# Small tiles moved behind the large ones: every large SBUF tile starts on a multiple of 512 bytes

## The chip, the cores and the metric

One core of one Trainium2 chip runs the whole program in one launch. The metric is the device time of that core in microseconds (us).

## The reference, cut to what matters

Two layers over x (256 positions, 1,024 channels, float32), each of three sub-layers with an RMS norm before and after:

```python
for i in range(DEPTH):                      # 2
    h = swiglu(rms_norm(x, g[0]), w_gate, w_up, w_down)      # D_FF = 2816
    x = x + 0.5 * rms_norm(h, g[1])
    hm = rms_norm(x, g[2])
    m = dilated_attention(hm, ...) if i == 0 else retention(hm, ...)
    x = x + rms_norm(m, g[3])
    h = swiglu(rms_norm(x, g[4]), w_gate, w_up, w_down)
    x = x + 0.5 * rms_norm(h, g[5])
```

Every weight is read once from HBM, and every product with a weight has 256 rows, so the work is one long stream of weights through TensorE.

## The kernel before, in words

**The weight stream.** Class `Stream` (L26 to L131) loads weights in groups of 1 MB into tiles `raw` (two buffers, 8,192 bytes per partition), issued by SP in `dma`. `split` cuts a group into two pieces of 128x1024 and writes each piece twice: ScalarE makes `hi` (L109, L115), rounded to fp32r, and VectorE makes the rest, `lo` (L110, L116). The pieces lie in rings of six tiles each, tags `whi` and `wlo`. When a piece has been used, `done` makes the next. Fourteen pieces at the borders of the sub-layers go to the idle tags C0, C1 and C2 instead (`wx`; `run` lists them, three per border and two behind the attention).

**The products.** `mm3` (L182 to L184) multiplies in three passes: (x high, w high), (x high, w low), (x low, w high). In each the 128x128 block of x is the stationary operand, loaded into the array by an LDWEIGHTS of its own, and 512 columns of the weights are the moving one. A triple below is these three. x high and x low are `xh` and `xl` in the first product of each sub-layer, `hh` and `hl` (tags A and B) in the down products of the feed-forward parts, `ot` (tags E0, E1 and C0) in the attention's output product, and `zh` and `zl` (tags A and B) in the retention's. Counted from the loops, there are 5,160 such matmuls: 4 x 528 in the feed-forward units (result tiles `ac`), 864 in the attention's (`at`), 768 in the retention's (`rt`), 4 x 264 + 96 + 192 = 1,344 in the down products (`d_f`, `d_at`, `d_rt`), and 72 in `rt_y` (tile `y`), where the stationary operand is `s` (tags x0 and x1) and the moving one `vv` (tag C1). Of those in the units, 14 x 12 = 168 have a `wx` as moving operand. Transposes, scores and softmax are separate matmuls of other lines.

**The order of the work.** It is the program's order on each queue; `enter` and the tail of `down` fix the order of PE, DVE and ACT by hand. Piece by piece, PE consumes what ACT and DVE have split; a piece ahead is split when one is done with.

**Where the tiles lie.** All SBUF tiles come from one pool, `sb` (L148). A tag's place is given when its first tile is asked for, one behind the other, each size rounded up to 32 bytes; the pool begins at byte 4,224 of the partition, which is 128 behind a multiple of 512. The large tiles have sizes that are multiples of 512, but tiles of 4 to 128 bytes (`rstd`, `ss2`, `nwt`, `pn`, `m`, `den`, ...) and `gcol` (384 bytes) lie between them. Adding up the sizes gives these starts, as the rest by 512:

| tiles | before | after |
|---|---|---|
| x0, x1 (also `s`), sg, raw, ident | 128 | 0 |
| xh, xl (blocks of x within them at 0 or 256) | 0 | 0 |
| whi, wlo | 64 | 0 |
| tmpa, pr | 128 | 0 |
| gpost, A, B (hh, hl, zh, zl, PT), E0, E1 (ot), C0, C1, C2 (wx, vv, qk), h, D | 224 | 0 |
| tmpb | 320 | 0 |

Of the kernel before, what the change touches and what calls it, by code (L numbers as in the profile page):

```python
# [6 lines left out]
F32 = mybir.dt.float32  # L7
# [7 lines left out]
P = 128  # L15
# [125 lines left out]
class Trunk:  # L141
    def __init__(self, tc, aps, out, ctx):
        self.tc, self.nc, self.out = tc, tc.nc, out
        self.__dict__.update(aps)
        self.pend = []
        self.bg = []
        self.begun = False
        self.sb = ctx.enter_context(tc.tile_pool(name="sb", bufs=1))  # L148
        self.ps = ctx.enter_context(tc.tile_pool(name="ps", bufs=6, space=PSUM))
        self.pt = ctx.enter_context(tc.tile_pool(name="pt", bufs=2, space=PSUM))  # L150
        self.dram = ctx.enter_context(tc.tile_pool(name="dram", bufs=1, space=DRAM))
# [6 lines left out]

    def setup(self):
        nc, sb = self.nc, self.sb  # L160

        self.x = [sb.tile([P, D], F32, tag=f"x{t}", name=f"x{t}") for t in range(2)]
        xr = self.x_in[0].rearrange("(i r) d -> r i d", r=4)
        gr = sb.tile([96, P], F32, tag="sg", bufs=2, name="gr")
        nc.sync.dma_start(gr, self.norm_gains.rearrange("l n (k p) -> (l n k) p", p=P))
        for t in range(2):
            for rr in range(2):
                nc.sync.dma_start(self.x[t][rr * 64 : rr * 64 + 64, :], xr[2 * t + rr])
            self.ws.dma(halves=t == 0)
        self.ident = sb.tile([P, P], F32, name="ident")  # L170
        make_identity(nc, self.ident)
        warm = self.acc("warm")
        for _ in range(WARM):
            nc.tensor.matmul(warm[:, :P], self.ident, self.ident, start=True, stop=True)
        tr = self.trb("gtr")
        nc.tensor.transpose(tr[:, :96], gr, self.ident[:96, :96])
        self.gcol = sb.tile([P, 96], F32, name="gcol")
        nc.vector.tensor_copy(self.gcol, tr[:, :96])

    def mm3(self, out, xh, xl, wh, wl, start, stop):  # L180
# [22 lines left out]
    def rsqrt(self, ss, name, mean, out=None):  # L203

        nc, n = self.nc, ss.shape[1]
        t = self.sb.tile([P, 4 * n], F32, tag="nwt%d" % n, bufs=3, name=f"nw_{name}")
        v, y, u, r = (t[:, i * n : i * n + n] for i in range(4))
        nc.vector.tensor_scalar(out=v, in0=ss, scalar1=mean, scalar2=EPS, op0=ALU.mult, op1=ALU.add)
        self.newton(v, y, u)
        r = r if out is None else out  # L210
        nc.vector.tensor_scalar(out=r, in0=y, scalar1=1.0 / NEWTON, scalar2=None, op0=ALU.mult)
        return r
# [14 lines left out]
    def pre_alloc(self, name):  # L227
        self.xh = self.sb.tile([P, NK, XC], F32R, tag="xh", name=f"xh_{name}")
        self.xl = self.sb.tile([P, NK, XC], F32R, tag="xl", name=f"xl_{name}")
        self.rstd = self.sb.tile([P, 2], F32, tag="rstd", bufs=2, name=f"rstd_{name}")  # L230

    def pre_sums(self, name, t, ss=None):
        if ss is None:
            ss = self.sb.tile([P, 2], F32, tag="ss2", bufs=2, name=f"ss_{name}")
        junk = self.sb.tile([P, D], F32, tag="tmpa", bufs=1, name=f"sq_{name}_{t}")
        if name == "in":
            self.nc.vector.scalar_tensor_tensor(out=junk, in0=self.x[t], scalar=1.0, in1=self.x[t], op0=ALU.mult, op1=ALU.mult, accum_out=ss[:, t : t + 1])
        else:
            self.nc.scalar.activation(junk, self.x[t], AF.Square, accum_out=ss[:, t : t + 1])
        return ss  # L240
# [7 lines left out]
    def post(self, t, banks, gb, name):  # L248

        nc, sb = self.nc, self.sb  # L250
        w = sb.tile([P, 5], F32, tag="pn", bufs=3, name=f"pn_{name}_{t}")
        junk = sb.tile([P, 512], F32, tag="tmpb", bufs=1, name=f"psq_{name}_{t}")
        yg = sb.tile([P, D], F32, tag="tmpa", bufs=1, name=f"yg_{name}_{t}")
        for h in range(2):
            s = slice(h * 512, h * 512 + 512)
            nc.scalar.activation(junk, banks[h], AF.Square, scale=2.0**-5, accum_out=w[:, h : h + 1])
            nc.vector.tensor_tensor(out=yg[:, s], in0=banks[h], in1=gb[:, s], op=ALU.mult)
        v, y, u = (w[:, i : i + 1] for i in (2, 3, 4))
        nc.vector.scalar_tensor_tensor(out=v, in0=w[:, 0:1], scalar=EPS, in1=w[:, 1:2], op0=ALU.add, op1=ALU.add)
        self.newton(v, y, u)  # L260
        for h in range(2):
            s = slice(h * 512, h * 512 + 512)
            nc.vector.scalar_tensor_tensor(out=self.x[t][:, s], in0=yg[:, s], scalar=y, in1=self.x[t][:, s], op0=ALU.mult, op1=ALU.add)
# [266 lines left out]
    def attn(self, plan, nxt):  # L530
        nc, sb = self.nc, self.sb
# [3 lines left out]
        rq = ru = None  # L535
        tasks_o1 = None
        for u, (o, kind, g, pieces) in enumerate(plan["units"]):
# [2 lines left out]
                bias, loads = self.bias_load(o)  # L540
            if u == 0:
                self.first_unit(pieces, accs)
                rq = sb.tile([P, 2], F32, tag="rq", name="rq")
                nc.vector.tensor_scalar(out=rq, in0=self.rstd, scalar1=-0.125, scalar2=None, op0=ALU.mult)
                for z in (self.xh, self.xl):
                    nc.gpsimd.tensor_copy(z[:, :, 256:320], z[:, :, 0:64].bitcast(F32))
                tr = self.trb("rut")
                nc.tensor.matmul(tr[0:64, 0:2], self.ident[:, 64:128], self.rstd, start=True, stop=True)
                nc.tensor.matmul(tr[64:128, 0:2], self.ident[:, 0:64], self.rstd, start=True, stop=True)
                ru = sb.tile([P, 2], F32, tag="ru", name="ru")  # L550
                nc.vector.tensor_copy(ru[0:64, :], tr[0:64, 0:2])
                nc.vector.tensor_copy(ru[64:128, 0:1], tr[64:128, 1:2])
                nc.vector.tensor_copy(ru[64:128, 1:2], tr[64:128, 0:1])
            else:
                for _ in range(2):
                    if loads:
                        loads.pop(0)()
                self.unit(pieces, accs, cols=(64, 192) if (kind == "v" and g == 2) else (0, P))
            if kind != "v":
# [4 lines left out]
                w = 0 if kind == "q" else 1  # L564
# [3 lines left out]
                    self.pend.append(lambda t=t, nat=nat, dst=qk[g][:, w, :, t * P : (t + 1) * P], u=u, w=w: self.qk_store(t, nat, dst, u, w == 0))  # L568
                if kind == "k" and g == 2:
                    st = dict(o=o, qk=qk, bias=bias, PT=sb.tile([P, 16, 384], F32, tag="B", name=f"PT{o}"),  # L570
                              den=sb.tile([P, 2, 16], F32, tag="den", bufs=2, name=f"den{o}"))

                    def push(st=st):
                        n = 8
                        for j in range(n + 2):
                            def step(j=j):
                                if j < n:
                                    self.sm_scores(st, j)
                                if 1 <= j <= n:
                                    self.sm_exp(st, j - 1)  # L580
                                if j >= 2:
                                    self.sm_trans(st, j - 2)
                            self.bg += [step, lambda: None]
                    self.pend.append(push)
# [49 lines left out]
    def sm_scores(self, st, j):  # L634


        nc, sb = self.nc, self.sb
# [13 lines left out]
        for s in range(2):  # L651
            i = 2 * j + s
            pr = sb.tile([P, 384], F32, tag="pr", bufs=6, name=f"pr{st['o']}_{i}")
            m = sb.tile([P, 1], F32, tag="m", bufs=6, name=f"m{st['o']}_{i}")
            nc.vector.tensor_tensor_reduce(
                out=pr.rearrange("p (b c) -> p b c", c=64), in0=sc[s][:, :384].rearrange("p (b c) -> p b c", c=64),
                in1=st["bias"][:, 4 * T : 4 * T + 6, i % 8, :], scale=1.0, scalar=3.0e38, op0=ALU.add, op1=ALU.min, accum_out=m)
            st["pr", i], st["m", i] = pr, m
# [206 lines left out]
    def rt_gate(self, st, d, sg):  # L865

        nc, sb = self.nc, self.sb
        h = st["h"]
        mv = sb.tile([P, 2, 2], F32, tag="mv", bufs=2, name=f"mv{h}{d}")
        for t in range(2):  # L870
            bs = sb.tile([P, 6], F32, tag="bs", bufs=2, name=f"bs{h}{d}{t}")
            nc.vector.bn_stats(out=bs, in_=st["y", d][t])
            nc.vector.bn_aggr(out=mv[:, t, :], in_=bs)
        r = self.rsqrt(mv[:, :, 1], f"gn{h}{d}", 1.0)
        for t in range(2):
            if d == 0:
                w = st["C2"][:, 512 * t : 512 * t + 512]
# [82 lines left out]
```

## Time and profile before

| | us |
|---|---|
| median of 3 runs | 1318.09 (1317.95 to 1318.52) |
| the profiled execution, its own time | 1317.18 |
| its span, first to last instruction | 1315.1 |
| PE busy | 1298.9 |
| VectorE (DVE) busy | 864.7 |
| ScalarE (ACT) busy | 712.1 |

The profile is one execution; 2.1 us of its own time lie outside the span. Matmuls overlap in the records: one of 512 columns is shown as some 390 to 400 ns long, while the next begins some 230 ns after it. So the busy share of PE and a matmul's length say little of its rate; the distance from one start to the next does, and the timeline shows it, in hundredths of a microsecond.

### The profile page before, as it was taken

How to read it: one execution, taken by the hardware profiler on the slowest of the kernel's cores; microseconds unless marked ns; L12 is line 12 of the kernel's file. 1: busy time of each engine (PE TensorE's matmuls, PEld its weight loads, DVE VectorE, ACT ScalarE, POOL GpSimd, SP SyncE). 2: the span in 40 equal slices, each digit the busy share in tenths (PEclk: the TensorE clock that was granted, in tenths of full speed). 3: DMA queues.
4: the chain of work that ended last, by engine and by line, in shares of the span. 5: the costliest groups of instructions: out<-in, count | busy, mean ns of one | idle time of the engine just before them, and what ended most of it. 6: DMA issues, size and time to landing. Idle time of an engine off the chain costs nothing.

```text
span 1315.1 us, 16640 instructions
## 1 busy us (share of the span) xinstructions
PE 1298.9 (99%) x6326; PEld 1051.8 (80%) x6326; DVE 864.7 (66%) x1541; ACT 712.1 (54%) x1103; POOL 19.4 (1%) x16
## 2 busy tenths in 40 slices
PE   8999999999999999999999999999999999999997
PEld 6878887877887778888888888877888887888886
DVE  5765547678467768765476665588787875766544
ACT  4655444566555658764455654455554545565532
POOL 1000001000000000000000000000000000000000
PEclk9999999999999999999999999999999999999999
DMA  7755467855864346554546555545454545565551
GB/s 214 235 183 192 173 212 183 203 192 147 204 179 158 129 149 227 192 192 173 184 162 227 170 189 192 192 144 185 152 175 145 176 160 192 166 202 183 172 190 64
DMA packets 129691, 235.45 MB, mean 179 GB/s; under 512 B 25019, under 2 KB 41899, under 8 KB 129612
## 3 DMA queue, kind: packets, MB, share of 16 engines
q1 hardware_dynamic: 129468, 234.14, 56.0%
q8 instruction: 49, 0.80, 0.2%
q10 hardware_dynamic: 144, 0.26, 0.1%
q14 instruction: 30, 0.25, 0.1%
HBM read 232.21 MB, written 1.12 MB: 177 GB/s over the span
## 4 chain that ended last, share of the span: by engine, by line
PE 90%; DVE 4%; DMA 3%; ACT 2%; issue 1%; SPq 0%; DVEq 0%; ACTq 0%
PE ac_f L184 12%; PE ac_f L183 12%; PE ac_f L182 12%; PE d_f L182 6%; PE d_f L184 6%; PE d_f L183 6%; PE at L182 5%; PE at L184 5%; PE at L183 5%; PE rt L184 4%; PE rt L183 4%; PE rt L182 4%; PE htr L340 1%; DMA raw<-in_ret_w_in_dram 1%; DMA raw<-in_ffn_w_gate_dram 1%; PE ptt L676 1%
## 5 line engine op out<-in xcount | busy, mean ns | idle before, releaser
L116 DVE SCALAR_TENSOR_TENSOR wlo<-raw,gcol,whi 128x512 fp32r<-128x512 f32 x596 | 417.2, 747 | 191.2 <-ACT whi L115 190.6
L115 ACT ACTIVATE whi<-raw,gcol 128x512 fp32r<-128x512 f32 x596 | 393.8, 715 | 273.2 <-PE ac_f L184 87.1
L110 DVE TENSOR_TENSOR wlo<-raw,whi 128x1024 fp32r<-128x1024 f32 x112 | 137.2, 1225 | 144.9 <-ACT whi L109 144.7
L109 ACT ACTIVATE whi<-raw 128x1024 fp32r<-128x1024 f32 x112 | 118.7, 1060 | 172.2 <-PE d_f L184 103.3
L182 PE MATMUL d_f<-whi,hhf 128*128 128x512 f32 x352 | 140.7, 400 | 0.0
L184 PE MATMUL d_f<-whi,hlf 128*128 128x512 f32 x352 | 138.8, 394 | 0.0
L183 PE MATMUL d_f<-wlo,hhf 128*128 128x512 f32 x352 | 138.2, 393 | 0.0
L182 PE MATMUL at<-whi,xh_f 128*128 128x512 f32 x276 | 111.6, 404 | 0.0
L184 PE MATMUL at<-whi,xl_f 128*128 128x512 f32 x276 | 108.3, 392 | 0.0
L183 PE MATMUL at<-wlo,xh_f 128*128 128x512 f32 x276 | 107.4, 389 | 0.0
L183 PE MATMUL rt<-wlo,xh_f 128*128 128x512 f32 x244 | 97.1, 398 | 0.0
L182 PE MATMUL rt<-whi,xh_f 128*128 128x512 f32 x244 | 96.7, 396 | 0.0
L184 PE MATMUL rt<-whi,xl_f 128*128 128x512 f32 x244 | 96.4, 395 | 0.0
L184 PEld LDWEIGHTS d_f<-whi,hlf 128*128 128x128 f32 x352 | 66.1, 188 | 17.1
L183 PEld LDWEIGHTS d_f<-wlo,hhf 128*128 128x128 f32 x352 | 66.1, 188 | 15.4
L182 PEld LDWEIGHTS d_f<-whi,hhf 128*128 128x128 f32 x352 | 66.1, 188 | 15.1
L182 PE MATMUL ac_f<-whi,xh_in 128*128 128x512 f32 x176 | 70.4, 400 | 2.2 <-ACT whi L115 1.9
L183 PE MATMUL ac_f<-wlo,xh_in 128*128 128x512 f32 x176 | 69.1, 392 | 1.2 <-DVE wlo L116 1.2
L184 PE MATMUL ac_f<-whi,xl_in 128*128 128x512 f32 x176 | 69.3, 394 | 0.0
L184 PE MATMUL ac_f<-whi,xl_at 128*128 128x512 f32 x168 | 66.2, 394 | 0.0
L182 PE MATMUL ac_f<-whi,xh_at 128*128 128x512 f32 x168 | 65.8, 393 | 0.2 <-ACT xh_at L224 0.2
L183 PE MATMUL ac_f<-wlo,xh_at 128*128 128x512 f32 x168 | 65.9, 392 | 0.0
(290 smaller groups left out, 2162.8 us busy)
## 6 DMA issues: line engine op xcount, KB each, us to landing
raw<-in_ffn_w_down_dram SPq DMA_DIRECT2D x44, 1024.0 KB, 4.9
raw<-in_ffn_w_up_dram SPq DMA_DIRECT2D x40, 1024.0 KB, 5.1
raw<-in_ffn_w_gate_dram SPq DMA_DIRECT2D x39, 1024.0 KB, 5.1
raw<-in_attn_w_in_dram SPq DMA_DIRECT2D x36, 1024.0 KB, 5.2
raw<-in_ret_w_in_dram SPq DMA_DIRECT2D x24, 1024.0 KB, 5.4
raw<-in_ret_w_in_dram SPq DMA_DIRECT2D x16, 512.0 KB, 4.6
raw<-in_ret_w_out_dram SPq DMA_DIRECT2D x8, 1024.0 KB, 4.9
raw<-in_ffn_w_gate_dram SPq DMA_DIRECT2D x10, 512.0 KB, 4.1
```

Of the source, the lines that this page charges most:

```text
L109: nc.scalar.activation(hi, raw, AF.Copy)
L110: nc.vector.tensor_tensor(out=lo, in0=raw, in1=hi.bitcast(F32), op=ALU.subtract)
L115: nc.scalar.activation(hi[:, s], raw[:, s], AF.Copy, scale=gc)
L116: nc.vector.scalar_tensor_tensor(out=lo[:, s], in0=raw[:, s], scalar=gc, in1=hi[:, s].bitcast(F32), op0=ALU.mult, op1=ALU.subtract,)
L182: mm(out, xh, wh, start=start, stop=False)
L183: mm(out, xh, wl, start=False, stop=False)
L184: mm(out, xl, wh, start=False, stop=stop)
L340: nc.tensor.transpose(tr[:, k * P : (k + 1) * P], h[:, k * P : (k + 1) * P], self.ident)
L676: self.nc.tensor.transpose(tr[:, c * P : (c + 1) * P], pr[:, c * P : (c + 1) * P], self.ident)
```

## The change

It makes a second pool, `sm`, behind `sb`, and takes ten tags of small tiles from it. It asks for `gcol` first of all, so that its 384 bytes fill the space up to byte 4,608, a multiple of 512. No instruction is added or taken out, and the copy that fills `gcol` stays where it was. Cut to its core (the other eight, `ss2`, `pn`, `rq`, `ru`, `den`, `m`, `mv` and `bs`, are edited as the two here):

```diff
@@ __init__
         self.sb = ctx.enter_context(tc.tile_pool(name="sb", bufs=1))
+        self.sm = ctx.enter_context(tc.tile_pool(name="sm", bufs=1))
@@ setup
         nc, sb = self.nc, self.sb
+
+        self.gcol = sb.tile([P, 96], F32, name="gcol")
...
         nc.tensor.transpose(tr[:, :96], gr, self.ident[:96, :96])
-        self.gcol = sb.tile([P, 96], F32, name="gcol")
         nc.vector.tensor_copy(self.gcol, tr[:, :96])
@@ rsqrt
-        t = self.sb.tile([P, 4 * n], F32, tag="nwt%d" % n, bufs=3, name=f"nw_{name}")
+        t = self.sm.tile([P, 4 * n], F32, tag="nwt%d" % n, bufs=3, name=f"nw_{name}")
@@ pre_alloc
-        self.rstd = self.sb.tile([P, 2], F32, tag="rstd", bufs=2, name=f"rstd_{name}")
+        self.rstd = self.sm.tile([P, 2], F32, tag="rstd", bufs=2, name=f"rstd_{name}")
...
```

## Rows read from the trace of the kernel before

**Rows 1.** The page: span, and busy time of each engine.
```profile
span 1315.1 us, 16640 instructions
...
PE 1298.9 (99%) x6326; PEld 1051.8 (80%) x6326; DVE 864.7 (66%) x1541; ACT 712.1 (54%) x1103; POOL 19.4 (1%) x16
...
PEclk9999999999999999999999999999999999999999
```

**Rows 2.** The page: the chain that ended last, by engine.
```profile
PE 90%; DVE 4%; DMA 3%; ACT 2%; issue 1%; SPq 0%; DVEq 0%; ACTq 0%
```

**Rows 3.** Waits in total, times, longest: ACT's in the down products.
```profile
ACT whi L109 <- PE d_f L184: 103.3, 60, 1.7
```

**Rows 4.** PE's timeline in a down product: start, length, what (60 matmuls apart).
```profile
164.73 0.40 PE L182 MATMUL d_f<-whi,hhf 128*128 128x512 f32 x1
...
178.73 0.40 PE L182 MATMUL d_f<-whi,hhf 128*128 128x512 f32 x1
```

**Rows 5.** PE's timeline, unit of layer 2: 18, then 15 matmuls apart.
```profile
679.04 0.40 PE L182 MATMUL ac_f<-wx,xh_f 128*128 128x512 f32 x1
...
683.24 0.39 PE L182 MATMUL ac_f<-whi,xh_f 128*128 128x512 f32 x1
...
686.68 0.39 PE L182 MATMUL ac_f<-whi,xh_f 128*128 128x512 f32 x1
```

**Rows 6.** PE's timeline, retention: 9 matmuls apart, y, then 26 apart.
```profile
891.99 0.39 PE L182 MATMUL rt<-whi,xh_f 128*128 128x512 f32 x1
...
894.05 0.39 PE L182 MATMUL rt<-whi,xh_f 128*128 128x512 f32 x1
...
894.51 0.39 PE L182 MATMUL y<-vv,s 128*128 128x512 f32 x1
...
896.84 0.40 PE L182 MATMUL rt<-whi,xh_f 128*128 128x512 f32 x1
...
902.90 0.40 PE L184 MATMUL rt<-whi,xl_f 128*128 128x512 f32 x1
```

**Rows 7.** Groups by line and shape: the smallest tiles' commonest instruction.
```profile
L194 DVE SCALAR_TENSOR_TENSOR pn_f<-pn_f 128x1 f32<-128x1 f32 x24 | 5.3, 220 | 0.9
```

**Rows 8.** Groups by line and shape: the split, on DVE and ACT.
```profile
L116 DVE SCALAR_TENSOR_TENSOR wlo<-raw,gcol,whi 128x512 fp32r<-128x512 f32 x596 | 417.2, 747 | 191.2 <-ACT whi L115 190.6
L115 ACT ACTIVATE whi<-raw,gcol 128x512 fp32r<-128x512 f32 x596 | 393.8, 715 | 273.2 <-PE ac_f L184 87.1 <-PE rt L184 54.2 <-PE at L184 29.7
...
L116 DVE SCALAR_TENSOR_TENSOR wx<-raw,gcol,wx 128x512 fp32r<-128x512 f32 x28 | 19.4, 748 | 7.3 <-ACT wx L115 7.3
L115 ACT ACTIVATE wx<-raw,gcol 128x512 fp32r<-128x512 f32 x28 | 18.3, 714 | 9.4 <-DMA raw<-in_ffn_w_gate_dram 5.6 <-DMA raw<-in_ret_w_in_dram 2.7 <-DMA raw<-in_attn_w_in_dram 1.2
```

**Rows 9.** Groups by line and shape: weight loads.
```profile
L182 PEld LDWEIGHTS d_f<-whi,hhf 128*128 128x128 f32 x352 | 66.1, 188 | 15.1
...
L182 PEld LDWEIGHTS ac_f<-whi,xh_at 128*128 128x128 f32 x168 | 31.6, 188 | 7.5 <-ACT xh_at L224 0.7
```

**Rows 10.** Groups by line and shape: matmuls of the down products and of y.
```profile
L182 PE MATMUL d_f<-whi,hhf 128*128 128x512 f32 x352 | 140.7, 400 | 0.0
...
L182 PE MATMUL d_rt<-whi,zh 128*128 128x512 f32 x64 | 25.7, 401 | 0.0
...
L182 PE MATMUL d_at<-whi,ot 128*128 128x512 f32 x32 | 12.9, 402 | 0.0
...
L182 PE MATMUL y<-vv,s 128*128 128x512 f32 x24 | 9.5, 396 | 0.0
```

**Rows 11.** The page: DMA queue of SP (packets, MB, share of 16 engines).
```profile
q1 hardware_dynamic: 129468, 234.14, 56.0%
```

More of the change, by code (lines that the diff above doesn't have):

```diff
@@ L229, in pre_alloc @@
         self.xl = self.sb.tile([P, NK, XC], F32R, tag="xl", name=f"xl_{name}")
-        self.rstd = self.sb.tile([P, 2], F32, tag="rstd", bufs=2, name=f"rstd_{name}")
+        self.rstd = self.sm.tile([P, 2], F32, tag="rstd", bufs=2, name=f"rstd_{name}")
     def pre_sums(self, name, t, ss=None):
         if ss is None:
-            ss = self.sb.tile([P, 2], F32, tag="ss2", bufs=2, name=f"ss_{name}")
+            ss = self.sm.tile([P, 2], F32, tag="ss2", bufs=2, name=f"ss_{name}")
         junk = self.sb.tile([P, D], F32, tag="tmpa", bufs=1, name=f"sq_{name}_{t}")
@@ L250, in post @@
         nc, sb = self.nc, self.sb
-        w = sb.tile([P, 5], F32, tag="pn", bufs=3, name=f"pn_{name}_{t}")
+        w = self.sm.tile([P, 5], F32, tag="pn", bufs=3, name=f"pn_{name}_{t}")
         junk = sb.tile([P, 512], F32, tag="tmpb", bufs=1, name=f"psq_{name}_{t}")
@@ L542, in attn @@
                 self.first_unit(pieces, accs)
-                rq = sb.tile([P, 2], F32, tag="rq", name="rq")
+                rq = self.sm.tile([P, 2], F32, tag="rq", name="rq")
                 nc.vector.tensor_scalar(out=rq, in0=self.rstd, scalar1=-0.125, scalar2=None, op0=ALU.mult)
@@ L549, in attn @@
                 nc.tensor.matmul(tr[64:128, 0:2], self.ident[:, 0:64], self.rstd, start=True, stop=True)
-                ru = sb.tile([P, 2], F32, tag="ru", name="ru")
+                ru = self.sm.tile([P, 2], F32, tag="ru", name="ru")
                 nc.vector.tensor_copy(ru[0:64, :], tr[0:64, 0:2])
@@ L570, in attn @@
                     st = dict(o=o, qk=qk, bias=bias, PT=sb.tile([P, 16, 384], F32, tag="B", name=f"PT{o}"),
-                              den=sb.tile([P, 2, 16], F32, tag="den", bufs=2, name=f"den{o}"))
+                              den=self.sm.tile([P, 2, 16], F32, tag="den", bufs=2, name=f"den{o}"))
                     def push(st=st):
@@ L653, in sm_scores @@
             pr = sb.tile([P, 384], F32, tag="pr", bufs=6, name=f"pr{st['o']}_{i}")
-            m = sb.tile([P, 1], F32, tag="m", bufs=6, name=f"m{st['o']}_{i}")
+            m = self.sm.tile([P, 1], F32, tag="m", bufs=6, name=f"m{st['o']}_{i}")
             nc.vector.tensor_tensor_reduce(
@@ L868, in rt_gate @@
         h = st["h"]
-        mv = sb.tile([P, 2, 2], F32, tag="mv", bufs=2, name=f"mv{h}{d}")
+        mv = self.sm.tile([P, 2, 2], F32, tag="mv", bufs=2, name=f"mv{h}{d}")
         for t in range(2):
-            bs = sb.tile([P, 6], F32, tag="bs", bufs=2, name=f"bs{h}{d}{t}")
+            bs = self.sm.tile([P, 6], F32, tag="bs", bufs=2, name=f"bs{h}{d}{t}")
             nc.vector.bn_stats(out=bs, in_=st["y", d][t])
```

## The prediction

> **What bounds the kernel.** [...] The chain that ended last is PE for 90% of the time [rows 2]. So the time is the number of matmuls times the distance from one start to the next, and whatever changes that distance counts in full, while DVE, ACT and the DMA have slack. In the down products ACT even waits 103.3 us for PE to free a piece [rows 3]: a faster PE finds its weights there.
>
> Next I read PE's timeline, not for lengths but for distances. They have two levels.
> - Down product: 60 matmuls in 178.73 - 164.73 = 14.00 us, **233.3 ns** each [rows 4].
> - A feed-forward unit that starts on spare pieces: 18 matmuls on wx in 683.24 - 679.04 = 4.20 us, 233.3 ns each; from the very next matmul, on whi, 15 in 3.44 us, **229.3 ns** each [rows 5]. Nothing else changes at that border: same xh, same lines, no wait between.
> - Retention: 9 in 2.06 us, 228.9 ns each, before a y; behind the y the same operands (whi, xh) take 6.06 us for 26, 233.1 ns each [rows 6].
>
> Laid beside the tile starts, the slow level stands wherever one operand starts 32 bytes off a multiple of 64: hh, zh and ot as stationary operands and wx and vv as moving ones all start at 224 = 3 x 64 + 32. The fast level stands only where both are multiples of 64 (whi at 64, xh at 0 or 256). The reverse does not hold: behind a y, aligned operands stay at the slow level until transposes come between. So the level has a memory; a misaligned operand sets it, and it may outlast that operand.
>
> **The change part by part.**
>
> *No instruction moves.* The count of 16640 [rows 1] should stay, with SP's and POOL's DMAs and operations in their order. Asking for gcol earlier gives only an address. I cost this at nothing.
>
> *Small tiles.* Their instructions, such as 24 of 128x1 at 220 ns [rows 7], read and write other addresses of the same alignment by 32. They lie beside matmuls except at the borders of sub-layers. Nothing; were a price of 10 ns hidden there, some 20 in a row at each of 5 borders would make 1 us.
>
> *ACT and DVE.* Rows exist on both sides of a misalignment: the split into wx (224) takes 748 ns on DVE and 714 on ACT, that into whi and wlo (64) 747 and 715 [rows 8]. Nothing, and what there is lies under PE.
>
> *Weight loads.* 188 ns from hh at 224 and 188 from xh at 0 or 256 [rows 9]. So the record of the load does not show the step; the distance between matmuls does.
>
> *Matmuls.* The step is 233.3 - 228.9 = 4.4 ns a matmul. Whom it concerns:
> - down products: 3 x (352 + 64 + 32) = 1,344 [rows 10] x 4.4 ns = 5.9 us;
> - wx: 14 pieces x 12 = 168 x 4.4 ns = 0.7 us;
> - y: 3 x 24 = 72 [rows 10] x 4.4 ns = 0.3 us;
> - rt behind a y: of 226 undisturbed triples on whi that I counted in the timeline, 133 stand at the slow level as in [rows 6]: 399 x 4.4 ns = 1.8 us. This goes only if y no longer sets the level.
>
> Sum: **8.7 us**, on PE's path, none of it hidden. I leave out the first 25 us, where aligned operands also run at the slow level (about 60 matmuls, 0.3 us): they are aligned now and so get no reason to change.
>
> *What no row shows* is a moving operand on a multiple of 128: whi moves from 64 to 0, and all 5,160 matmuls read at such a place. Bounds: another step of the same size down, 5,160 x 4.4 ns = 22.7 us less; or a step up for those at the fast level now (5,160 - 1,344 - 72 - 168 - 399, less 60, so 3,117), 13.7 us more. I take nothing, because the nearest rows, 64 and 0 or 256 together, already run at the fast level and xh on a multiple of 256 is no faster than that. Both ends stay in the range.
>
> *Transfers.* raw moves from 128 to 0. SP's queue takes 56.0% of 16 DMA engines' time [rows 11], and DMA is 3% of the chain [rows 2], some 39 us. No row shows a transfer to another alignment of raw, so: nothing by the trace; if it were worth a twentieth of the exposed transfers, 2 us either way. [...]
>
> The profiled execution took 1317.18 us, 0.9 below the median of 1318.09. 1317.2 - 8.7 = 1308.5 against that execution, so **1309.4** against the median.
>
> **The rivals.** About 0.2%, 2.6 us, is what a measurement of this kernel can tell from no change.
>
> *Nothing changes: 1318.1.* The two levels would be a matter of phase alone: what a stage's pattern of operands or result banks sets, with the alignment a coincidence. For it: aligned operands hold the slow level too, behind y and at the start. Against it: the border in [rows 5], where the moving tile alone changes, and that all the down products, with three different stationary tiles, show 233 ns. Had the memory alone set the level, transposes inside the down products would have let it fall, as they do in rt. [...]
>
> *Slower: 1331.8.* All operands now start at the same rest by 512, so the loads of the stationary block and the stream of the moving one could meet where 64 bytes keep them apart today, and the slow level would become that of ac, at and rt. Its place is the 3,117 matmuls above, its price 13.7 us over the median. It decides if ac's matmuls on whi stand 233 ns apart in the changed timeline. For it: aligned operands can hold the slow level at all. Against: xh's blocks alternate between 0 and 256 while whi stays at 64, so two distances between the operands have been tried, and the fast level held at both.
>
> *Much faster: 1286.7.* The fast level itself still holds a step, of whi at 64: 22.7 us beyond nothing, with the 8.7 us 31.4. [...] Against: stationary blocks at 0 and 256, in place today, show no third level.
>
> *Half of it: 1312 to 1314.* The memory outlives the alignment and the down products stay slow in part. I count this with the forecast.
>
> **How the numbers follow.** Forecast, whole or in part: 0.50, at 1306 to 1314. Nothing: 0.20. Slower: 0.16, of which 0.06 for a part of the stages only, below 1323. Much faster: 0.14, of which 0.04 for a part of the matmuls only, above 1300. Faster by over 0.2% is 0.50 + 0.14 = 0.64, the same 0.20, slower 0.16. The range 1300 to 1323 leaves out the rest of these two, 0.10 + 0.10, 2 in 10; it takes in the 2 us of the transfers and the 1 us of the small tiles. The forecast's own range, with the sum's parts each right or wrong, is 1306 to 1314.
>
> **What would show it.** In the changed profile the timeline of a down product should have 60 matmuls in 13.73 us, not 14.00, and a unit's first 18 on wx 4.12 us, not 4.20; rt should hold 229 ns behind a y; ac should stay at 229. The groups of DVE, ACT and weight loads should keep their means to a few ns, and the count of instructions should be 16640. The prediction is wrong if the down products stay at 233 (then the alignment was no cause), if ac or at leave 229 either way (then the place modulo 128 or more matters), or if PE's gain returns as idle time before matmuls, waiting for ACT, DVE or raw.

## The result, and the profile after

The changed kernel took **1302.72 us** (median; 1302.60 to 1303.39 in 4 runs) where the kernel before took 1318.3: a ratio of 0.9883 [0.9868, 0.9898] (in brackets, here and below, the 95% interval), 15.6 us less. The forecast was 1309.4, the range 1300 to 1323: the direction and the range held, and the gain was nearly twice the sum of 8.7 us.

The page after, in the columns of [rows 1] and [rows 11]: span and busy time of the engines, the granted clock by slices, SP's DMA queue.

```profile
span 1300.5 us, 16640 instructions
...
PE 1283.4 (99%) x6326; PEld 1052.9 (81%) x6326; DVE 864.5 (66%) x1541; ACT 711.9 (55%) x1103; POOL 19.8 (2%) x16
...
PEclk8999999999999999999999999999999999999999
...
q1 hardware_dynamic: 129468, 234.14, 55.6%
```

The count is the same, DVE and ACT are within 0.2 us, and all that left the span (14.6 us) left PE (15.5 us). Where on PE? The timeline of the down product that answers to [rows 4], 60 matmuls from the first row to the second, then the unit of layer 2 that answers to [rows 5] (18 on `wx`, then 15 on `whi`), then the retention behind a y, which answers to the last two of [rows 6] (24 matmuls here):

```profile
162.98 0.39 PE L184 MATMUL d_f<-whi,hhf 128*128 128x512 f32 x1
...
176.58 0.39 PE L184 MATMUL d_f<-whi,hhf 128*128 128x512 f32 x1
...
672.66 0.39 PE L184 MATMUL ac_f<-wx,xh_f 128*128 128x512 f32 x1
...
676.74 0.39 PE L184 MATMUL ac_f<-whi,xh_f 128*128 128x512 f32 x1
...
680.14 0.39 PE L184 MATMUL ac_f<-whi,xh_f 128*128 128x512 f32 x1
...
889.27 0.39 PE L184 MATMUL rt<-whi,xh_f 128*128 128x512 f32 x1
...
894.71 0.39 PE L184 MATMUL rt<-whi,xh_f 128*128 128x512 f32 x1
```

That is 13.60 us for 60, 4.08 for 18, 3.40 for 15 and 5.44 for 24: **226.7 ns** each, in all four places. Before they were at 233.3, 233.3, 229.3 and 233.1 [rows 4, 5, 6]. The slow level went, as forecast; but the fast level of before, 229, went too, and that was not forecast.

A mean of all the distances of up to 260 ns between matmuls of `mm3` (some 4,970 of 5,160; longer ones hold a wait or other work) gives the whole account:

```
            before   after   difference   matmuls   us
d (down)    233.3    226.9      6.4        1,344     8.6
ac          229.3    227.1      2.2        2,112     4.6
at          229.4    227.9      1.5          864     1.3
rt          231.6    227.1      4.5          768     3.5
y           232.6    227.5      5.1           72     0.4
                                                    18.4
```

Over the 4,970 that can be measured it is 17.8 us. The span is only 14.6 us shorter, so some 3.2 us were lost again elsewhere. Two places show most of it. The first is the end of the second feed-forward part, in PE's timeline around the transposes there (in brackets the idle time ahead of a row and what ended it), then in DVE's:

```profile
848.81 0.39 PE L186 MATMUL d_f<-whi,hlf 128*128 128x512 f32 x1
850.47 1.29 PE L222 MATMUL xtr_f<-ident,xn 128*128 128x128 f32 x8 [1.28 <-DVE xn L265]
```

```profile
844.41 2.74 DVE L116 SCALAR_TENSOR_TENSOR wx<-raw,gcol,wx 128x512 fp32r<-128x512 f32 x4 [2.53 <-ACT wx L115]
...
849.58 1.41 DVE L265 SCALAR_TENSOR_TENSOR xn<-yg_f,pn_f,xn 128x512 f32<-128x512 f32 x2
```

And the chain of waits of that stretch, start, length and what:

```profile
837.04 6.52 DMA raw<-in_ret_w_in_dram
...
843.65 0.73 ACT wx L115
...
844.41 2.75 DVE wx L116 x4
```

Read backwards: the transposes wait for `xn`, `xn` stands on DVE behind the split of four halves of pieces into `wx`, the split waits for a transfer of 6.52 us. In the kernel before, the same transposes begin 0.32 us after the start of the matmul ahead of them (here 1.66), and that transfer took 5.61 us. Its chain of waits, then the first row of the transposes in PE's timeline, and then the same transfer in run 5 below, which is slower than the kernel before:

```profile
845.71 5.61 DMA raw<-in_ret_w_in_dram
```

```profile
858.23 1.29 PE L220 MATMUL xtr_f<-ident,xn 128*128 128x128 f32 x8
```

```profile
852.89 7.30 DMA raw<-in_ret_w_in_dram
```

From the transfer's start to the transposes 12.52 us pass before and 13.43 here: 0.91 more, all of it the longer transfer. Only the other 0.4 of the 1.34 us is PE arriving sooner. The runs below say the same: the gap was 0.23 us behind a transfer of 5.52 (run 4), and 2.07 us behind the 7.30 of run 5, where PE is slow. So most of this wait is not the price of a faster PE. Why the transfer took longer, no run here shows. The second place is the start, the mean clock and the DMA share of 6 us of it (busy time and instructions of each engine, then PEclk, DMA share, GB/s), here and before:

```profile
7.00:13.00 6.00, 4.33 (x11) 2.96 (x10) 4.12 (x6) 3.53 (x6) 0.00 (x0) 0.58 1.05 292
```

```profile
7.00:13.00 6.00, 3.52 (x12) 2.06 (x13) 4.08 (x6) 3.32 (x6) 0.00 (x0) 1.00 1.04 244
```

PE idled 1.67 us for the first weights (1.50 before), and the next twelve matmuls ran at a lower granted clock (a mean of 0.58 in this stretch), from the third on some 427 ns apart; the second block of transposes of x begins at 14.49 us where it began at 13.20. These two places make 2.6 of the 3.2 us; the rest I did not trace. The start is not shown to be a property of the change. The profiles of the runs below are also one execution each, and this block begins at 13.25 us in run 2 and at 14.15 in run 3, with the same time in the end. (The clock of this view is to be read with care so early: it says 0.72 for run 2 and 1.00 for run 3, but run 3's matmuls too stand some 427 ns apart, from 10.73 to 12.86 us.)

The groups of the other engines, as [rows 7, 8, 9]:

```profile
L116 DVE SCALAR_TENSOR_TENSOR wlo<-raw,gcol,whi 128x512 fp32r<-128x512 f32 x596 | 417.9, 749 | 184.3 <-ACT whi L115 183.5
...
L184 PEld LDWEIGHTS d_f<-whi,hhf 128*128 128x128 f32 x352 | 66.1, 188 | 13.5
...
L196 DVE SCALAR_TENSOR_TENSOR pn_f<-pn_f 128x1 f32<-128x1 f32 x24 | 5.3, 220 | 0.9
```

749 ns, 188 and 220 against 747, 188 and 220: nothing moved but the distance between matmuls.

### The profile page after: what moved, and what is told of

The parts are those of the page before. It is cut to its first block, busy times and chain, and to the rows that moved or that the text cites. A ratio compares the mean times of both kernels' runs of the same rounds, so it can differ in the third digit from the quotient of the medians.

```text
span 1300.5 us, 16640 instructions
## 1 busy us (share of the span) xinstructions
PE 1283.4 (99%) x6326; PEld 1052.9 (81%) x6326; DVE 864.5 (66%) x1541; ACT 711.9 (55%) x1103; POOL 19.8 (2%) x16
## 4 chain that ended last, share of the span: by engine, by line
PE 90%; DVE 4%; DMA 3%; ACT 2%; issue 1%; SPq 0%; DVEq 0%; ACTq 0%
PE ac_f L184 12%; PE ac_f L185 12%; PE ac_f L186 12%; PE d_f L184 6%; PE d_f L186 6%; PE d_f L185 6%; PE at L184 5%; PE at L186 5%; PE at L185 5%; PE rt L186 3%; PE rt L185 3%; PE rt L184 3%; DMA raw<-in_ret_w_in_dram 2%; PE htr L342 1%; DVE wlo L116 1%; PE ptt L678 1%
## 5 line engine op out<-in xcount | busy, mean ns | idle before, releaser
L109 ACT ACTIVATE whi<-raw 128x1024 fp32r<-128x1024 f32 x112 | 118.8, 1061 | 165.3 <-PE d_f L186 101.2
L184 PE MATMUL d_f<-whi,hhf 128*128 128x512 f32 x352 | 137.6, 391 | 0.0
```

The costliest lines, as they stand in the source:

```text
L109: nc.scalar.activation(hi, raw, AF.Copy)
L184: mm(out, xh, wh, start=start, stop=False)
```

## The experiments

The question was what an operand's place has to do with the distance between matmuls. The prediction said: each operand's own place, 32 off a multiple of 64 is bad. Rivals: the alignment to 512; and the distance between the two operands, the start of the moving one less that of the stationary one. The edits put unused tiles ("pads") ahead of a tag, so that all that follows moves, and change no instruction. Two kinds of distance occur: in ns, from the start of one matmul to the start of the next, and in bytes, between the starts of the two operands. The second is given by its rest by 256 (what is left when multiples of 256 are taken off), so "at 64" means that the moving operand starts 64 bytes behind the stationary one by that rest. Ratios are to the kernel before, timed beside each run (1317.65 to 1319.01 us).

**1. The rings 64 further (`e1_whi64`).** All else stays at multiples of 512.

```diff
         self.rstd = self.sm.tile([P, 2], F32, tag="rstd", bufs=2, name=f"rstd_{name}")
+        self.pad(64, "pad_whi")
...
+        self.pad(448, "pad_tmpa")
```

> The changed kernel with whi and wlo alone moved up by 64 bytes (a pad before them, one of 448 bytes behind them), all else on multiples of 512. Place theory (what counts is where each operand starts: 226.7 ns from matmul to matmul with both on multiples of 128 or more, 228.9 with one on an odd multiple of 64, 233.3 with one 32 off): ac, at, rt and the down products all go from 226.7 to 228.9 ns, some 5,000 x 2.2 ns = 11 us, so 1312 to 1314 us. Distance theory (what counts is the distance between the two operands' places): the same here. Phase theory (alignment of 64 or more is nothing to PE, the step below 229 ns came from something else): 1302.7 us and 226.7 ns stay.

Measured: 1310.67 us, ratio 0.9943 [0.9928, 0.9958]. PE's timeline, 30 matmuls of a unit and 60 of a down product:

```profile
65.58 0.39 PE L191 MATMUL ac_f<-wlo,xh_in 128*128 128x512 f32 x1
...
72.45 0.39 PE L191 MATMUL ac_f<-wlo,xh_in 128*128 128x512 f32 x1
...
151.23 0.39 PE L191 MATMUL d_f<-wlo,hhf 128*128 128x512 f32 x1
...
164.97 0.39 PE L191 MATMUL d_f<-wlo,hhf 128*128 128x512 f32 x1
```

229.0 in both, and the time lies below the 1312 to 1314 expected. At 64 the three matmuls of a triple are not alike: from the first, second and third of them to the next start it is 231.4, 227.0 and 229.5 ns (means over the units), and 229 is their mean. So the fast level of before was the price of the 64 bytes between `whi` and its partner, and a third, faster level lies at 0. This run is also the prediction's forecast without its surprise: no operand 32 off, no slow stage but the few y, and 1310.67 beside the forecast 1309.4.

**2 and 3. Everything at 64, everything at 32 (`e2_all64`, `e3_all32`).** One pad ahead of all large tiles, `self.pad(64, "pad_x0")` or 32: the distances between tiles stay those of the changed kernel, and no large tile begins on a multiple of 512.

> The changed kernel with every large tile moved up by 64 bytes (one pad in front), so that moving and stationary operands keep their distance. Place theory: 228.9 ns or more everywhere, 1312 to 1320 us. Distance theory: nothing changes, 226.7 ns and 1302.7 us. Phase theory: 1302.7 us too.

> The changed kernel with every large tile moved up by 32 bytes. Place theory: the slow level, 233.3 ns, in every stage, 5,160 x 6.6 ns = 34 us more, so about 1337 us. Distance theory: nothing changes, 226.7 ns and 1302.7 us.

Measured: 1301.82 us, 0.9883 [0.9867, 0.99], and 1303.25 us, 0.9887 [0.9872, 0.9902]. The spans of the two pages:

```profile
span 1299.8 us, 16640 instructions
```

```profile
span 1299.7 us, 16640 instructions
```

The same time as the change, at 32 off for every operand. That ends the prediction's rule of the operand's own place, and the alignment to 512 with it.

**4. The stationary tiles A and all behind them 32 further (`e4_stat32`).** `self.pad(32, "pad_A")` ahead of A: hh, zh and ot as stationary, wx and vv as moving operands are 32 off again; the units' own tiles are not.

> The changed kernel with all tiles from A on moved up by 32 bytes: hh, hl, zh, zl, ot (stationary in the down products) and wx, vv (moving at the borders and in y) stand 32 off, while whi, wlo, xh, xl and s stay on multiples of 512. Place theory and distance theory: the down products, wx and y go from 226.7 to 233.3 ns, 1,584 x 6.6 ns = 10.5 us, and up to 2.6 us in rt behind y, so 1312 to 1316 us, while ac and at stay at 226.7. Phase theory: 1302.7 us.

Measured: 1309.88 us, 0.9937 [0.9922, 0.9951]. PE's timeline, a unit, 30 apart, and a down product, 60 apart:

```profile
65.89 0.39 PE L191 MATMUL ac_f<-wlo,xh_in 128*128 128x512 f32 x1
...
72.72 0.39 PE L191 MATMUL ac_f<-wlo,xh_in 128*128 128x512 f32 x1
...
151.10 0.39 PE L191 MATMUL d_f<-wlo,hhf 128*128 128x512 f32 x1
...
165.09 0.40 PE L191 MATMUL d_f<-wlo,hhf 128*128 128x512 f32 x1
```

227.7 and 233.2: the slow level comes back where the two operands are 32 apart (by the rest by 64), and only there. The time is below the expected 1312: the retention behind a y hardly suffers (227.9 ns, mean of `rt`), and the gap of 1.66 us above is 0.23 here. With runs 2 and 3 this settles it: 32 off is slow beside 0, and fast beside 32.

**5. The rings 128 further (`g1_whi128`).** As run 1, with 128 and 384.

> The changed kernel with whi and wlo alone moved up by 128 bytes, all else on multiples of 512. The theory after the first four runs: what counts is the distance between the places of the moving and the stationary operand; 0 or 256 gives 226.8 ns from matmul to matmul, an odd multiple of 64 gives 229, 32 off gives 233.3. If 128 is as good as 0 (the distance counts modulo 128), 226.8 ns and 1302 to 1303 us; if it counts modulo 256, a level between 226.8 and 229, so 1303 to 1310 us. A rival, that the whole gain over 229 ns needs the large tiles on multiples of 512 as the title says, is gone already with all tiles at 32 or 64.

Measured: 1326.09 us, 1.0053 [1.0036, 1.007], slower than the kernel before, with every operand on a multiple of 128. Both cases of the expectation, 1302 to 1310 us, were wrong. PE's timeline, 30 matmuls of a unit:

```profile
66.39 0.39 PE L191 MATMUL ac_f<-wlo,xh_in 128*128 128x512 f32 x1
...
73.36 0.39 PE L191 MATMUL ac_f<-wlo,xh_in 128*128 128x512 f32 x1
```

232.3 ns. A good alignment of each operand is worth nothing by itself.

**6. Only x low 32 further (`g2_xl32`).** `self.pad(32, "pad_xl")` ahead of `xl`, 480 behind it. In a triple the third matmul alone has a stationary block 32 off; it is loaded while the second one streams.

> The changed kernel with xl alone moved up by 32 bytes. In a triple only the third matmul has a stationary operand 32 off; its weights are loaded while the second one streams. If the load meets the stream of the matmul before, the distance from the second matmul's start to the third's grows to 233 ns or more and the others stay; if what counts is the third's own stream, the third's distance grows. In either case ac, at and rt (3,744 matmuls) lose a third to all of 6.6 ns each, 8 to 25 us, so 1310 to 1327 us, and the down products stay at 226.8 ns. Rival, that only a steady offset of all operands sets the slow level: 1303 us.

Measured: 1321.5 us, 1.0021 [1.0012, 1.003]. PE's timeline, a triple and the beginning of the next, in a unit:

```profile
67.70 0.39 PE L190 MATMUL ac_f<-whi,xh_in 128*128 128x512 f32 x1
67.93 0.40 PE L191 MATMUL ac_f<-wlo,xh_in 128*128 128x512 f32 x1
68.17 0.39 PE L192 MATMUL ac_f<-whi,xl_in 128*128 128x512 f32 x1
68.39 0.40 PE L190 MATMUL ac_f<-whi,xh_in 128*128 128x512 f32 x1
68.63 0.40 PE L191 MATMUL ac_f<-wlo,xh_in 128*128 128x512 f32 x1
```

And from the timeline of the weight loads, that of the shifted block:

```profile
67.93 0.19 PEld L192 LDWEIGHTS ac_f<-whi,xl_in 128*128 128x128 f32 x1
```

From each row to the next: the mean over the units is 232.2 ns from the first of a triple (L190), 238.7 from the second (L191), 228.7 from the third (L192). The third, which alone multiplies with the shifted block, is the quickest of them; the second, under which that block is loaded (its load begins with it, at 67.93), is the slowest. So the stream seems to lose time to the load of the next block, not to its own. But the first pays too, with both its neighbours at distance 0, and that no run explains.

**7. The kernel before, with two pads (`g3_before_pads`).** No second pool, no gcol moved: 448 bytes ahead of the rings and 352 ahead of gpost bring their distances to 0; raw and x stay at 128.

```diff
+        self.pad(448, "pad_whi")
...
+        self.pad(352, "pad_gpost")
```

> The kernel before, with its small tiles left between the large ones in one pool, and two unused pads: 448 bytes before whi and 352 before gpost. So whi, wlo and everything from gpost to C2 lie on multiples of 512 like xh and xl, while x0, x1, raw and ident stay at 128, tmpa at 64 and pr at 416. Distance theory: the whole gain, 1302 to 1304 us, without a second pool. Rival, that the gain needs raw or the other large tiles on multiples of 512 (transfers, DVE and ACT), or the small tiles elsewhere: 1306 to 1318 us.

Measured: 1302.27 us, 0.9878 [0.9863, 0.9893], as the change. PE's timeline, a down product (60 apart), then the retention straight behind a y, whose operands are 384 apart here (24 matmuls on `whi`):

```profile
149.26 0.40 PE L189 MATMUL d_f<-wlo,hhf 128*128 128x512 f32 x1
...
162.91 0.39 PE L189 MATMUL d_f<-wlo,hhf 128*128 128x512 f32 x1
...
887.93 0.39 PE L188 MATMUL rt<-whi,xh_f 128*128 128x512 f32 x1
...
893.37 0.39 PE L188 MATMUL rt<-whi,xh_f 128*128 128x512 f32 x1
```

227.5 in the down product, and 5.44 us for 24, 226.7, straight behind a y that ran at 234 (mean of its distances). At distance 0 the slow level did not outlast its cause here; at 64 it did (233.1 ns, [rows 6]). The run also bears on the transfers: raw begins 128 behind a multiple of 512 as in the kernel before, and nothing is lost by it.

**8. x high and x low 16 further (`g4_x16`).** Both in tiles 128 elements longer, written and read 4 elements in.

> The changed kernel with xh and xl read and written 16 bytes into longer tiles, so that the distance of the moving to the stationary operand is 16 off in ac, at and rt, and still 0 in the down products. Distance theory, if the level is set by the largest power of two that divides the distance (256, 64, 32: 226.8, 229, 233.3): 233 ns or more in ac, at and rt, 3,744 x 6.6 ns = 25 us or more, so 1327 us or above; if only the distance within 64 counts, as a share of it, between 226.8 and 233 ns, 1303 to 1327 us. [...]

Measured: 1314.04 us, 0.9965 [0.9952, 0.9978]. PE's timeline, two stretches of one unit, 30 matmuls each:

```profile
19.81 0.39 PE L191 MATMUL ac_f<-wlo,xh_in 128*128 128x512 f32 x1
...
26.61 0.39 PE L191 MATMUL ac_f<-wlo,xh_in 128*128 128x512 f32 x1
...
42.46 0.40 PE L191 MATMUL ac_f<-wlo,xh_in 128*128 128x512 f32 x1
...
49.46 0.39 PE L191 MATMUL ac_f<-wlo,xh_in 128*128 128x512 f32 x1
```

226.7 and 233.3 with operands whose starts have the same rests by 256, moving less stationary 240: at this distance both levels hold themselves, and the work that comes between (eight transposes from 41.35 us on) can flip them. This is the memory that the prediction saw in the retention. The expectation's first case, 1327 us or above by the largest power of two that divides the distance, did not come.

**9 and 10. Six distances in one ring (`h1_ring_a`, `h2_ring_b`).** The pieces lie in tiles 128 elements longer and begin at an offset that changes from piece to piece (in h2: 0, 24, 40, 8, 2 and 112 elements).

```diff
-            hi = self.K.sb.tile([P, 1024], F32R, tag="whi", ...)
+            o = (0, 48, 56, 4, 12, 60)[self.n_ring % 6]
+            self.n_ring += 1
+            hi = self.K.sb.tile([P, 1152], F32R, tag="whi", ...)[:, o : o + 1024]
```

> The changed kernel with the pieces whi and wlo read at byte 0, 192, 224, 16, 48 and 240 of their tiles in turn, so that the moving operand starts 0, 192, 224, 16, 48 or 240 bytes behind the stationary one (by the rest by 256) in ac, at and rt, twelve matmuls at a time. Theory (the distance between the two starts sets the time of a matmul): matmuls on pieces at 0 stand 227 ns apart; at 192, the mirror of 64, 229; at 224, as at 32, 233; for 16, 48 and 240 it says nothing, and 227 to 233 is left open. A mean of some 230 over 3,700 matmuls, against 227: about 11 us over the changed kernel, 1310 to 1320. Rival A (each operand's own place: a multiple of 64 is good, 32 off is bad): 227 at 0 and 192 alike, 233 at 224, 16, 48 and 240. Rival B (the level is a matter of phase and memory, and not of the pieces): no step at the borders between pieces; one level over many pieces.

> As the run before, with the pieces read at byte 0, 96, 160, 32, 8 and 448 of their tiles in turn. Theory (distance): 227 ns at 0; 233 at 96, 160 and 32; 229 at 448, which is 192 by the rest by 256; 8 left open between 227 and 233, and if any distance gives less than 226.7, it is here or in the run before. About 1312 to 1322 us. Rival A (place): 227 at 0 and 448, 233 at 96, 160, 32 and 8. Rival B (phase and memory): no step at the borders between pieces.

Measured, in one execution each: 1324.52 and 1328.8 us, beside 1317.65 for the kernel before: both slower than expected. Three pieces of a down product in PE's timeline of the first of them, at distance 240, 0 and 192: rows 1 to 2 are 11 matmuls at 240; rows 2 to 3 the first six at 0, rows 3 to 4 the last six; rows 4 to 5 twelve at 192.

```profile
153.03 0.40 PE L194 MATMUL d_f<-wlo,hhf 128*128 128x512 f32 x1
...
155.63 0.40 PE L193 MATMUL d_f<-whi,hhf 128*128 128x512 f32 x1
...
157.02 0.39 PE L193 MATMUL d_f<-whi,hhf 128*128 128x512 f32 x1
...
158.38 0.39 PE L193 MATMUL d_f<-whi,hhf 128*128 128x512 f32 x1
...
161.18 0.40 PE L193 MATMUL d_f<-whi,hhf 128*128 128x512 f32 x1
```

236.4, then 231.7 falling to 226.7, then 233.3 from the first matmul. The level follows the piece, so it is no matter of phase alone; and a piece at 0 needed some six matmuls to come down, which is why the pieces at 0 had a mean of 228.5 and 229.8 in the two runs. What the expectation had wrong was 192: taken for the mirror of 64, it ran at 233.

**11. The whole ring at 192 (`h3_whi192`).** As run 1, with 192 and 320, since on the mixed ring the memory of the pieces before might have made that 233.

> The changed kernel with the whi and wlo rings 192 bytes further, all else at multiples of 512: 4,920 matmuls have their moving operand 192 bytes behind the stationary one by the rest by 256 (or 64 ahead of it), the whole ring alike, so that no change of distance from piece to piece blurs the level. Theory as the two runs on mixed rings leave it (every distance has a level of its own, 64 bytes behind is not the mirror of 64 ahead): 233 ns in ac, at, rt and the down products, 4,900 x 6.2 ns = 30 us over the changed kernel's 1302.7, some 3 us of it taken back in waits that vanish: 1327 to 1333, ratio about 1.009. Rival (192 is as good as 64, and what the mixed rings showed at 192 was the memory of the pieces before): 229 ns, 1310 to 1312, ratio 0.994, as with the rings at 64.

Measured: 1329.41 us, 1.0091 [1.0074, 1.0107]. PE's timeline, 60 matmuls of a down product:

```profile
152.84 0.39 PE L191 MATMUL d_f<-wlo,hhf 128*128 128x512 f32 x1
...
166.84 0.39 PE L191 MATMUL d_f<-wlo,hhf 128*128 128x512 f32 x1
```

233.3 ns. So 64 behind (229.0 in run 1) is not 64 ahead, and the distance counts by the rest by 256 at least. The pieces in `wx` stand at 0 in this run, between pieces at 192: on them the distances come down to 227 ns within four to eleven matmuls, and behind the last of them they are at 233 again from the first matmul on `whi`. The runs together, mean distance of the matmuls in ns, with how many there were:

```
distance   held over whole stages            changing piece by piece
0          227.2 (4,968, the change)         228.5, 229.8
8                                            234.5
16                                           231.7
32         233.5 (228, run 4's wx and y)     232.9
48                                           231.3
64         229.2 (4,742, run 1)
96         233.3 (1,319, before's down)      234.4
128        232.5 (4,743, run 5)
160                                          233.9
192        233.3 (4,744, run 11)             233.3, 233.1
224        233.3 (1,319, run 4's down)       232.9
240        226.7 or 233.3 (run 8)            234.4
```

The means of the right column shift by some 0.3 ns with how the matmuls at the border of two pieces are counted, and each holds some of the memory of the piece ahead. A distance of 256 is as good as 0: in the changed kernel the blocks of x at 256 have a mean of 227.2, those at 0 of 227.4. No distance tried is better than 0, so no version came out that beats the change; runs 2, 3 and 7 equal it.

## Why the prediction was right or wrong

**What bounds the kernel: right.** PE's distance between matmuls counts in full, as 15.5 us less of PE's busy time in a span shorter by 14.6 show. The fall of ACT's wait from 103.3 us [rows 3] to 101.2 says that the slack was there. That none of the gain would be lost again was too much: 3.2 us were, in the profiled executions, of these 1.3 at the start and 0.9 by one transfer that took longer, and no run ties either to the change.

**The two levels: seen rightly, explained wrongly.** The step that failed is "the slow level stands wherever one operand starts 32 bytes off a multiple of 64". It fitted all the rows of before, since the starts of 224 happened to stand beside partners at 0, 64 and 128. Runs 2 and 3 (all at 64, all at 32: 1301.82 and 1303.25 us, no loss) and run 5 (all on multiples of 128: 1326.09 us, slower than before) put the distance between the operands in its place. That the direction came out is luck in part: the change brings every operand's own place and every distance to a multiple of 256 at once, so the wrong rule and the right one both forecast a gain from it; for run 5 the wrong rule sees nothing amiss, and it is the slower kernel. The prediction's own sign of being wrong, that ac or at leave 229 either way, did come (227 and 228), though the cause that it named with it, the place modulo 128 or more, is not the one either. The prediction could have asked what else changes at the border of [rows 5]: not only the place of the moving tile, also its distance from xh, from 224 to 64.

**The sum: two terms mis-sized, one missing.** Down products: 5.9 us by a step of 4.4 ns, measured 8.6 by 6.4 ns. Retention: 1.8 us for the matmuls behind a y; all of rt gained 3.5. The missing term is the fast level itself: the units' and the attention's gained 4.6 + 1.3 us, of which the sum had at most the 0.7 of the wx. The prediction bounded this by "another step of the same size down" and took nothing, "because the nearest rows, 64 and 0 or 256 together, already run at the fast level and xh on a multiple of 256 is no faster than that". That reason was void: 0 and 256 are one and the same distance, so only one distance had been tried. The right term was a step of some 2.2 ns, half of the bound's 4.4.

**The rivals.** "Nothing" fell: the phase does have a part (runs 8, 9 and 10 show a memory), but the level follows the place: runs 1, 4, 5 and 11, whose starts are all multiples of 32, hold levels up to 6 ns a matmul above the change's (229.2 to 233.5 against 227.2). "Slower" had its reason upside down: "the same rest by 512" for both operands was the best place tried, and times near its 1331.8 came only where the starts differ (1329.41 at 192, 1328.8 on run 10's mixed ring). "Much faster" named the right mechanism, a step left in the fast level, at twice its size. "Half of it" did not happen.

**Small tiles, ACT and DVE, weight loads, instructions: nothing, as said.** The rows above show it to 2 ns.

**Transfers: nothing, as said.** The change, runs 2, 3 and 7 have raw at 0, 64, 32 and 128 by the rest by 512, and 1302.72, 1301.82, 1303.25 and 1302.27 us. Run 7, with raw at 128 as in the kernel before, was 0.45 us faster than the change, with raw at 0. An interval of 2 us on each doesn't rule out a smaller effect, but no loss at 128 shows.

**What stays open.** Why the distance counts. Run 6 points to the stream of one matmul meeting the load of the next block. These runs show that the time from matmul to matmul hangs on where the one's operand starts as against the other's, by up to 6 ns in 227 over whole stages (227.2 at 0, 233.3 at 192), so the stream and the load are not independent in effect. What ties them, no run here shows.

## What to carry to other kernels

Where a kernel is bound by back-to-back matmuls, look at the distance from start to start by stage, not at busy time, and where it has levels, lay the starts of *both* operands beside them: here a moving operand that starts a multiple of 256 bytes from the stationary one gave 227 ns, any other distance tried 229 to 235, but for 240, which at times held 227. When a rule is read from a few coinciding addresses, first list which pairs have been seen; a pattern that held "at 0 and 256" had been tested once. And where a faster engine meets a new wait, look for the same wait in slower runs before calling it the price: here it went with the length of one transfer, and the longest, 2.07 us, was in a kernel slower than the one before.

## What the runs showed of the hardware that was not expected

- The time of a 128x128 by 128x512 matmul in fp32r depends on the distance of its operands' starts in SBUF: 226.7 ns at 0, 229 at 64, 232 to 234 at 32, 96, 128, 192 and 224, and it is not symmetric (64: 229, 192: 233).
- The levels have a memory. At distance 240 both 226.7 and 233.3 hold over 30 matmuls or more (run 8); at 64 a slow level outlasted its cause by 26 matmuls [rows 6]; at 0 it is gone at once (run 7) or after four to eleven matmuls (runs 9 and 11).
- None of this shows in the record of a weight load, which takes some 188 ns at every distance read (group means of 188 to 191 ns in the kernel before, the change and runs 1 to 10), and hardly in a matmul's length (group means of 389 to 406 ns).
